# Two chained two-layer models on one core: the modulation products keep to other stages, and the value products of the neighbourhood attention take their PSUM tiles from the projections' pool

## The chip, the cores and the metric

The kernel runs on one core of one Trainium2 chip. The metric is the device time of one execution in microseconds (us). The core has TensorE (PE, with its weight load PEld), VectorE (DVE), ScalarE (ACT), GpSimd (POOL), and SyncE (SP), whose queue issues most DMAs.

## The reference

`x` is 512 tokens by 1024 features. The first model has two layers, each of them a mixer, a cross-attention to 256 memory tokens and a feed-forward stage with a causal convolution of width 3. The second model has two layers too, with a context of 256 tokens beside `x`; its norms are modulated by vectors that are computed from `c` and `c_ctx`:

```python
for l in range(2):                                     # first model
    x = x + (even_mixer, odd_mixer)[l](rms(x, mix_g[l]))   # retention + HGRN2; dilated attention
    x = x + cross_attention(rms(x, xa_g[l]), rms(mem, xm_g[l]))
    gate, up = split(rms(x, ffn_g[l]) @ w_in[l])
    x = x + (gelu(causal_conv(gate)) * up) @ w_out[l]
for i in range(2):                                     # second model
    mod   = split6(silu(c)     @ ada_w[i] + ada_b[i])  # shift, scale, gate, twice: j = 0..5
    mod_c = split6(silu(c_ctx) @ ada_w[i] + ada_b[i])
    h, hc = modulate(rms(x), mod), modulate(rms(ctx), mod_c)
    y, yc = (ab_mixer, cd_mixer)[i](h, hc)             # token MLP + neighbourhood attention;
    x   = x + g_m * y                                  #   Fourier mix + gated linear attention
    x   = x + g_f * swiglu(modulate(rms(x), mod))
    if i == 0:                                         # the context runs to the end of layer 0
        ctx = ctx + gc_m * yc; ctx = ctx + gc_f * swiglu(modulate(rms(ctx), mod_c))
return rms(x)
```

In the neighbourhood attention every query attends to 8 rows of a grid 64 wide (16 columns of each) and to the 256 context tokens, with one softmax over both.

## The kernel before

**Layout and stages.** Activations lie feature-major, as 8 tiles of 128 features by 512 tokens in fp32. The stages follow each other as mix0, xa0, ffn0, mix1, xa1, ffn1 (first model), bm0, bf0, bm1, bf1, out (second model): mixers are mix0, mix1, bm0 and bm1, feed-forward stages ffn0, ffn1, bf0 and bf1. Every fp32 product is three matmuls in fp32r: high part by high part, high by low, low by high.

**Weight units.** A unit is 512 KB of weights: one DMA on SP's queue (4 buffers `wr`), a cast on ScalarE to the high part `wh` (L303, 3 buffers), a subtraction on VectorE for the low part `wl` (L304, 3 buffers), and then 24 matmuls of 128x512 into a PSUM tile. The matmuls' lines are L322, L352, L949, L1183, L1194 and L1208, one for each kind of projection.

**PSUM.** There are two pools of four banks. `PM()` gives the tiles `m` of projections, `PA()` the tiles `a` of everything else (attention logits, transposes, sums over features, broadcasts).

**The modulation products.** The vectors `mod` and `mod_c` of both layers are 12 products (l = 0, 1; j = 0 to 5). Each reads 16 tiles of 256 KB from `w_ada` through SP's queue and accumulates on VectorE: L1070 for the first tile of a half, L1072 for the seven others, once per stream (both streams for l = 0 and for j below 2). Then VectorE transposes and sums (L1076, L1078), one small matmul folds the parts (L452), and VectorE adds the bias (L1082). The generator `side()` runs this a step at a time: each weight unit calls `tick()`, and `tick()` takes one step. `finish_side(l)` takes all steps that are left of layer l.

**Order.** The program emits its instructions in the order of the Python code; `weave()` interleaves attention units with background jobs; a scheduler then fixes the order on each engine when the program is built. On the chip every engine takes its instructions in that order.

**The places that the change touches.** In mix0 the first eight input tiles are squared and summed on GpSimd (L523, L525), and the sum is folded over features by TensorE (L427), which the norm needs. Later in mix0 the gates of the HGRN2 heads (L578 to L588) feed prefix products over time, called trees here: TensorE's L601 starts each of them, VectorE's L611 and L612 carry them. At the end of ffn1 VectorE adds the result to x (L931) and, in the norm's sum (L438), the squares of eight tiles; TensorE's L427 folds that sum, while L1208 (the context's value projection of bm0) lies between. In bm0 a unit of neighbourhood attention (`attend`, from L1340 on) makes logits (L1351), a softmax on ACT and DVE (L1253 to L1261, L1355, L1359), transposes (L1365) with their copies to SBUF (L1367), and value products `po` (L1373); projections (L1183) are the background jobs. At the border from bf0 to bm1 the last matmuls of bf0 are left as 12 jobs, which cd_mixer emits together with the first steps of `modulate` for x. Those steps are the fold (L427), its result to all partitions (L490, L1099) and the modulated tiles (L1112, L1113, L1120; the odd ones by L1108 to L1118).

Of the kernel before, what the change touches and what calls it, by code (L numbers as in the profile page):

```python
# [235 lines left out]
class Net:  # L236
    def __init__(self, ctx, tc, a):
        self.tc, self.nc, self.a = tc, tc.nc, a
        E = ctx.enter_context
        self.cp = E(tc.tile_pool(name="cp", bufs=1))  # L240
        self.xp = E(tc.tile_pool(name="xp", bufs=9))
        self.cx = E(tc.tile_pool(name="cx", bufs=9))
        self.A = E(tc.tile_pool(name="A", bufs=NSLOT))
        self.sp = E(tc.tile_pool(name="sp", bufs=40))
        self.wr = E(tc.tile_pool(name="wr", bufs=4))
        self.wh = E(tc.tile_pool(name="wh", bufs=3))
        self.wl = E(tc.tile_pool(name="wl", bufs=3))
        self.pm = E(tc.tile_pool(name="pm", bufs=4, space=PSUM))
        self.pa = E(tc.tile_pool(name="pa", bufs=4, space=PSUM))
        self.dp = E(tc.tile_pool(name="dp", bufs=1, space=bass.MemoryType.DRAM))  # L250
        self.n = 0
        self.side = None
        self.early = []
        self.consts()
# [117 lines left out]
    def tick(self):  # L372
        if self.side is not None and next(self.side, None) is None:
            self.side = None
# [139 lines left out]
    def even_mixer(self, x, filler):  # L514
# [4 lines left out]
        for k in range(8):  # L519
            xs.append(self.split(x[k], scale=self.V("mixg0", k)))  # L520
            self.fm2_step(first, xs, k)
            sq = acc if k == 0 else self.T()
            nc.gpsimd.tensor_tensor(sq, x[k], x[k], ALU.mult)  # L523
            if k:
                nc.gpsimd.tensor_tensor(acc, acc, sq, ALU.add)  # L525
# [193 lines left out]

        hv, rv, sc, ri, gates = [], [], {}, {}, {}  # L720
        inp = {0: hg_inputs(0)}
        self.mem_prep()
# [21 lines left out]
        for h in range(4):  # L744
            jobs.append(lambda h=h: retention(h, *ri[h]))
            if h < 2:
                jobs.append(lambda h=h: ret_in(h + 2))
        self.weave(trees(), jobs, depth=4, rate=0.75)
        extra = []
        jobs = iter(filler(extra))  # L750
# [149 lines left out]
    def conv_ffn(self, l, x, st, xs, gain=None, mid=None):  # L900
# [21 lines left out]
        for p, (lo, hi) in enumerate(PARTS):  # L922
# [3 lines left out]
            for m in range(8):  # L926
                if mid is not None and p > 0:
                    next(mid, None)
                ps = self.fm1(f"w_fo{l}", m * 3 + p, hid[lo:hi])
                t = self.xp.tile([128, 512], F32, tag="x", name=f"x{self.n}")  # L930
                nc.vector.tensor_add(t, ps, x[m])  # L931
                out.append(t)
                if p == 2:
                    if gain is not None:
                        nxt.append(self.split(t, scale=self.V(gain, m)))
                    self.stat_add(st, m, t)
            x = out
        return x, st, nxt

# [13 lines left out]
    def odd_mixer(self, x, st, xs, filler):  # L953
# [17 lines left out]
        p = {}  # L971
# [63 lines left out]
        ff = filler(extra)  # L1035
        jobs = jobs[:12] + ff[:1] + jobs[12:17] + ff[1:3] + jobs[17:] + ff[3:]
        self.weave(units(), jobs, depth=3, rate=0.85)
        return self.residual("w_odo", ys, x, "xag1"), extra

# [11 lines left out]
    def ada(self, l, j):  # L1051
# [5 lines left out]
        for half in range(2):  # L1057
# [16 lines left out]
            for i in ids:  # L1074
                tr = self.T()
                nc.vector.transpose(tr, acc[i])  # L1076
                o = (i * 2 + half) * 16
                nc.vector.tensor_reduce(part[:, o:o + 16], tr.rearrange("p (b t) -> p b t", t=32), AX.X, ALU.add)  # L1078
        ps = self.PA()
        self.fold(ps, part, w, 1)  # L1080
# [105 lines left out]
    def dxs(self, wts, xs, n=512, pss=None, s=None):  # L1186

        pss = pss or [self.PM() for _ in wts]
        s = s or slice(0, n)
        for j, (xh, xl) in enumerate(xs):  # L1190
            ws = slice(j * 128, j * 128 + 128)
            for ps, wt in zip(pss, wts):
                for i, (A, B) in enumerate(((wt[0], xh), (wt[0], xl), (wt[1], xh))):
                    self.nc.tensor.matmul(ps[:, s], A[:, ws], B[:, s], start=j == 0 and i == 0, stop=j == len(xs) - 1 and i == 2)  # L1194
        return pss

    def tm_c(self, w, g, cs, evac):
# [74 lines left out]
    def ab_mixer(self, x, st, c, cs):  # L1272
# [73 lines left out]
        def attend(hp, i, logits, nbias, vals, yh, yl, n, order):  # L1346
# [22 lines left out]
            yield  # L1369
            po = self.PA()  # L1370
            for s, vv in enumerate(vals):
# [190 lines left out]
    def cd_mixer(self, r):  # L1562
# [3 lines left out]
        mx = self.modulate(x, r["sx"], 1, 0, 0, xs)  # L1566
        for i, job in enumerate(r["jobs"]):
            job()
            if i in (2, 5):
                next(mx, None)  # L1570
        self.run(mx)
        SCf, SCb = self.T(), self.T()
# [32 lines left out]
        qs, ks, kcs = [], [], []  # L1605
        pq = self.dxs([self.wt("w_cd", m) for m in range(2)], xs)
        self.run(mc)
        for m in range(2):
# [310 lines left out]
def body(ctx, tc, a, stop=None, start=None):  # L1919
# [32 lines left out]
    def side(ls):  # L1952
# [4 lines left out]
        for l in ls:  # L1957
            for j in range(6):
                for _ in k.ada(l, j):
                    for _ in range(2 - l):  # L1960
                        yield True

    def finish_side(l):
        while (l, 5) not in k.done:
            k.tick()
# [3 lines left out]
    def context():  # L1969
        load("c")  # L1970
        yield
        finish_side(0)
        yield from k.ctx_in(c, cs)
# [24 lines left out]
    for step in STEPS[STEPS.index(start or "mix0"):]:  # L1998
# [6 lines left out]
        elif step == "mix1":  # L2005
            (x, st, xs), kv = k.odd_mixer(x, st, xs, lambda out: k.mem_kv(1, out))
        elif step == "bm0":
            r = k.ab_mixer(x, st, c, cs)
        elif step in ("bf0", "bf1"):
            r = k.swiglu(int(step[-1]), r)  # L2010
        elif step == "bm1":
            finish_side(1)
            r = k.cd_mixer(r)
# [27 lines left out]
```

## Time and profile before

| | |
|---|---|
| Median of 3 runs (lowest, highest) | 3136.11 us (3135.73, 3138.0) |
| The profiled execution, its span | 3135.71 us, 3133.4 us |
| TensorE busy, share of the span | 3082.6 us, 98% |
| VectorE, ScalarE, GpSimd busy | 1781.0, 1115.8, 424.6 us |
| DMA, mean over the span | 100 GB/s |

The span runs from the first to the last profiled event; the time of the execution is 2.3 us longer. All positions are microseconds from the span's start. A busy TensorE can still run at its lower clock, so busy time and granted clock are read together. `[1.00 <-POOL t L525]` behind an instruction says that its engine sat idle for 1.00 us before it, and that GpSimd's L525, which writes a tile t, ended that.

### The profile page before, as it was taken

The page shows a single profiled execution, that of the slowest core. Times are in us where ns is not written, and L with a number is a line of the kernel's source. Part 1 is how long each engine was busy: PE and PEld are TensorE (multiplying, and loading weights), DVE is VectorE, ACT ScalarE, POOL GpSimd, SP SyncE. Part 2 cuts the span into 40 slices and gives each one's busy share as a digit, 9 for nine tenths or more (in the row PEclk, how much of TensorE's full clock was granted, in tenths as well). Part 3 has the DMA queues.
Part 4 walks back from the last instruction along what each step waited for, and adds up shares of the span by engine and source line. Part 5 has one row for each costly group of instructions (what it writes and reads, how often), then busy time and mean ns, then how long its engine had stood idle before and what let it go on. Part 6 is the DMA issues. An engine that isn't in the chain of part 4 may idle for free. (4 is left out here: it accounts for less than half of the span.)

```text
span 3133.4 us, 41147 instructions
## 1 busy us (share of the span) xinstructions
PE 3082.6 (98%) x16364; PEld 2584.5 (82%) x16364; DVE 1781.0 (57%) x2916; ACT 1115.8 (36%) x1868; POOL 424.6 (14%) x369
## 2 busy tenths in 40 slices
PE   8999999999999999999999999999999999999998
PEld 6878888888877888888878777888888878888887
DVE  7767676565648767668663557443332463643333
ACT  2234353232445534423243544221212352442223
POOL 5023111010111121101021112000000310110001
PEclk9999999999999999999999999999999999999999
DMA  5224323333333422334443013232211131222232
GB/s 171 79 77 155 118 78 117 119 123 123 118 105 100 148 94 95 125 129 144 139 150 106 26 38 105 98 118 71 90 66 54 68 113 31 64 77 100 94 101 68
DMA packets 110354, 312.80 MB, mean 100 GB/s; under 512 B 12177, under 2 KB 17682, under 8 KB 110162
## 3 DMA queue, kind: packets, MB, share of 16 engines
q1 hardware_dynamic: 101968, 297.32, 28.2%
q10 hardware_dynamic: 8194, 12.86, 1.3%
q8 instruction: 129, 2.11, 0.3%
q14 instruction: 63, 0.52, 0.0%
HBM read 306.98 MB, written 3.15 MB: 99 GB/s over the span
## 5 line engine op out<-in xcount | busy, mean ns | idle before, releaser
L1183 PE MATMUL m<-t,wh 128*128 128x512 f32 (+1 forms) x3716 | 993.3, 354 | 1.1 <-DVE t L1120 0.4
L303 ACT CAST wh<-wr 128x1024 fp32r<-128x1024 f32 (+2 forms) x462 | 471.1, 1022 | 1203.5 <-PE m L1183 395.1
L304 DVE TENSOR_TENSOR wl<-wr,wh 128x1024 fp32r<-128x1024 f32 (+2 forms) x462 | 558.8, 1210 | 447.4 <-ACT wh L303 428.8
L322 PE MATMUL m<-t,wh 128*128 128x512 f32 (+1 forms) x2576 | 772.2, 382 | 0.0
L1183 PEld LDWEIGHTS m<-t,wh 128*128 128x128 f32 x3716 | 655.3, 189 | 105.6 <-issue 8.8
L1183 PE MATMUL m<-t,wl 128*128 128x512 f32 (+1 forms) x1858 | 656.0, 353 | 0.5 <-DVE wl L304 0.5
L322 PEld LDWEIGHTS m<-t,wh 128*128 128x128 f32 x2576 | 474.0, 188 | 89.9 <-issue 1.0
L322 PE MATMUL m<-t,wl 128*128 128x512 f32 (+1 forms) x1288 | 490.9, 381 | 0.0
L1183 PEld LDWEIGHTS m<-t,wl 128*128 128x128 f32 x1858 | 351.1, 189 | 49.6 <-issue 1.9
L322 PEld LDWEIGHTS m<-t,wl 128*128 128x128 f32 x1288 | 242.5, 188 | 45.9 <-issue 0.7
L438 POOL TENSOR_TENSOR t<-t,t 128x512 f32<-128x512 f32 (+1 forms) x90 | 112.2, 1250 | 1163.1 <-ACT t L433 1141.4
L1072 DVE SCALAR_TENSOR_TENSOR t<-t,silc,t 128x512 f32<-128x512 f32 x280 | 219.1, 811 | 14.7 <-DMA t<-w_ada 13.9
L949 PE MATMUL m<-t,wh 128*128 128x512 f32 x704 | 217.2, 390 | 0.0
L352 PE MATMUL m<-t,wh 128*128 128x512 f32 x496 | 158.9, 400 | 7.4 <-ACT wh L303 7.4
L949 PEld LDWEIGHTS m<-t,wh 128*128 128x128 f32 x704 | 131.8, 188 | 27.4
L411 ACT CAST t<-t 128x512 fp32r<-128x512 f32 x116 | 72.0, 621 | 189.7 <-DVE t L1547 104.4
L916 POOL TENSOR_TENSOR t<-t,t 128x512 f32<-128x512 f32 x44 | 64.5, 1467 | 549.7 <-ACT t L915 532.3
L949 PE MATMUL m<-t,wl 128*128 128x512 f32 x352 | 136.9, 389 | 0.0
L1453 DVE SCALAR_TENSOR_TENSOR x<-m,modt,x 128x512 f32<-128x512 f32 (+1 forms) x75 | 50.1, 671 | 142.4 <-PE m L1183 142.2
L421 POOL TENSOR_TENSOR s<-s,nh 128x4 f32<-128x4 f32 (+2 forms) x67 | 71.2, 1064 | 406.2 <-DVE s L483 154.5
L367 PE MATMUL m<-wh,t 128*128 128x512 f32 x384 | 123.1, 396 | 0.0
L352 PEld LDWEIGHTS m<-t,wh 128*128 128x128 f32 x496 | 93.3, 191 | 26.5 <-ACT wh L303 7.4
(391 smaller groups left out, 3602.5 us busy)
## 6 DMA issues: line engine op xcount, KB each, us to landing
t<-w_ada SPq DMA_DIRECT2D x192, 256.0 KB, 3.9
wr<-w_fi SPq DMA_DIRECT2D x88, 512.0 KB, 3.3
wr<-w_gu SPq DMA_DIRECT2D x88, 512.0 KB, 3.3
wr<-w_fo SPq DMA_DIRECT2D x32, 512.0 KB, 3.3
wr<-w_dn SPq DMA_DIRECT2D x32, 512.0 KB, 3.1
wr<-w_ev SPq DMA_DIRECT2D x24, 512.0 KB, 3.3
wr<-w_xk SPq DMA_DIRECT2D x16, 512.0 KB, 3.3
wr<-w_xv SPq DMA_DIRECT2D x16, 512.0 KB, 3.2
```

What stands on the lines that cost most here:

```text
L303: nc.scalar.copy(h[:, 0:e], r[:, 0:e])
L304: nc.vector.tensor_sub(lo[:, 0:e], r[:, 0:e], h[:, 0:e])
L322: nc.tensor.matmul(ps[:, 0:n], A[:, s], B[:, 0:n], start=c == 0, stop=c == tot - 1)
L352: self.nc.tensor.matmul(ps, A[:, s], B, start=k == 0 and i == 0, stop=k == K - 1 and i == 2)
L367: nc.tensor.matmul(pss[tb], A[:, ts], B[:, s], start=(u == 0 and j == 0 and i == 0), stop=(u == nu - 1 and j == kper - 1 and i == 2))
L411: nc.scalar.copy(h[:, 0:n], src[:, 0:n])
L421: self.nc.gpsimd.tensor_tensor(r, v, self.nh[:, 0:w], ALU.pow)
L438: e.tensor_tensor(st[0][:, 0:n], st[0][:, 0:n], sq[:, 0:n], ALU.add)
L916: nc.gpsimd.tensor_tensor(y, y, rb, ALU.mult)
L949: nc.tensor.matmul(ps[:, 0:n], A[:, s], B[:, 0:n], start=c == 0, stop=c == tot - 1)
L1072: nc.vector.scalar_tensor_tensor(acc[i], r, s, acc[i], ALU.mult, ALU.add)
L1183: nc.tensor.matmul(ps[:, s], A[:, ws], B[:, s], start=j == 0 and i == 0, stop=j == last and i == 2)
```

## The change

There are six parts.

1. A flag `quiet` makes `tick()` do nothing: in mix0 from before the memory's preparation to the end of the trees, in the weave of mix1, for the second half of the last pass of ffn0 and ffn1 (m above 3 of 8), and throughout bm0.
2. In mix0, the squares of the odd tiles are computed on ScalarE; the sums stay on GpSimd.
3. The modulation products get three empty steps ahead of the fold. `side()` spaces layer 0's steps by 2 and 1 ticks in turn (before: 2), and layer 1's by 0 and 1 (before: 1), so two steps may fall on one tick.
4. The context of bm0 waits for the first three products of layer 0 only, and bm1 for the first three of layer 1; bf0 and bf1 ask for the rest of theirs. In the built order none of these calls leaves a run of products at a border.
5. At the border to bm1, x's modulation is emitted in full after job 7 of the 12 jobs (before: its steps after the folds came behind all jobs). The context's modulation is emitted inside the first two projections of bm1, behind their input tiles 2 and 5.
6. In `attend`, the value products take their PSUM tile from `PM()` instead of `PA()`.

```diff
@@ tick @@
-        if self.side is not None and next(self.side, None) is None:
+        if self.side is not None and not self.quiet and next(self.side, None) is None:
@@ even_mixer @@
             sq = acc if k == 0 else self.T()
-            nc.gpsimd.tensor_tensor(sq, x[k], x[k], ALU.mult)
+            if k % 2:
+                nc.scalar.activation(sq, x[k], AF.Square)
+            else:
+                nc.gpsimd.tensor_tensor(sq, x[k], x[k], ALU.mult)
...
+        self.quiet = True
         inp = {0: hg_inputs(0)}
         self.mem_prep()
...
         self.weave(trees(), jobs, depth=4, rate=0.75)
+        self.quiet = False
@@ conv_ffn @@
                 if mid is not None and p > 0:
                     next(mid, None)
+                self.quiet = p == 2 and m > 3
...
+        self.quiet = False
@@ odd_mixer @@
+        self.quiet = True
         self.weave(units(), jobs, depth=3, rate=0.85)
+        self.quiet = False
@@ ada @@
+        for _ in range(3):
+            yield True
         ps = self.PA()
         self.fold(ps, part, w, 1)
@@ new @@
+    def between(self, steps, js):
+        for j in js:
+            with self.tc.issue_after(self.marks[j]):
+                next(steps, None)
+    def border(self, jobs, steps, at):
+        for i, job in enumerate(jobs):
+            job()
+            if i in at:
+                next(steps, None)
+            if i == at[-1]:
+                self.run(steps)
+        self.run(steps)
@@ attend @@
-            po = self.PA()
+            po = self.PM()
@@ cd_mixer @@
-        for i, job in enumerate(r["jobs"]):
-            job()
-            if i in (2, 5):
-                next(mx, None)
-        self.run(mx)
+        self.border(r["jobs"], mx, (2, 5, 7))
...
         pq = self.dxs([self.wt("w_cd", m) for m in range(2)], xs)
+        self.between(mc, (2, 5))
         self.run(mc)
@@ side, finish_side, context, the steps @@
-                for _ in k.ada(l, j):
-                    for _ in range(2 - l):
+                for i, _ in enumerate(k.ada(l, j)):
+                    for _ in range(i % 2 if l else 2 - i % 2):
                         yield True
-    def finish_side(l):
-        while (l, 5) not in k.done:
+    def finish_side(l, j=5):
+        while (l, j) not in k.done:
...
-        finish_side(0)
+        finish_side(0, 2)
...
         elif step == "bm0":
+            k.quiet = True
             r = k.ab_mixer(x, st, c, cs)
         elif step in ("bf0", "bf1"):
+            k.quiet = False
+            finish_side(int(step[-1]))
             r = k.swiglu(int(step[-1]), r)
         elif step == "bm1":
-            finish_side(1)
+            finish_side(1, 2)
```

No engine's count of these instructions changes but for the four squares; the 192 loads of `w_ada` are spread otherwise over the stages. In SP's order, ffn0 holds 36 of them before and 39 after, ffn1 52 and 64, bm0 16 and none, bf0 40 and 56.

VectorE at the end of ffn1, before; L1070 and L1072 are modulation products, L931 adds to x, L304 makes a unit's low part, and L438 is the last addition of the norm's sum:

```order
L1070 TENSOR_SCALAR t_13458<-t_13459,silc 128x512
L1072 SCALAR_TENSOR_TENSOR t_13458<-t_13461,silc,t_13458 128x512
L1072 SCALAR_TENSOR_TENSOR t_13458<-t_13463,silc,t_13458 128x512
L931 TENSOR_TENSOR x_13557<-m_13532,x_12802 128x512
L304 TENSOR_TENSOR wl_13650<-wr_13647,wh_13649 128x1024
L1072 SCALAR_TENSOR_TENSOR t_13458<-t_13496,silc,t_13458 128x512
L1072 SCALAR_TENSOR_TENSOR t_13458<-t_13529,silc,t_13458 128x512
L931 TENSOR_TENSOR x_13590<-m_13565,x_12842 128x512
L1072 SCALAR_TENSOR_TENSOR t_13458<-t_13562,silc,t_13458 128x512
L438 TENSOR_TENSOR t_13303<-t_13303,t_13592 128x512
```

The same place after, where L938 is the addition to x, L305 the low part and L439 the norm's addition:

```order
L938 TENSOR_TENSOR x_13510<-m_13485,x_12691 128x512
L305 TENSOR_TENSOR wl_13603<-wr_13600,wh_13602 128x1024
L938 TENSOR_TENSOR x_13540<-m_13515,x_12735 128x512
L305 TENSOR_TENSOR wl_13630<-wr_13627,wh_13629 128x1024
L938 TENSOR_TENSOR x_13570<-m_13545,x_12775 128x512
L305 TENSOR_TENSOR wl_13655<-wr_13652,wh_13654 128x1024
L439 TENSOR_TENSOR t_13294<-t_13294,t_13572 128x512
```

The modulation products have left the end of ffn1, and one low part more stands ahead of the norm's addition.

Earlier in ffn1, after, VectorE between two low parts (the first two rows of this stretch are L305's and an L413, then two L1080, and six more L1082 stand ahead of these; L1080 and L1082 are the products that were L1070 and L1072):

```order
L1082 SCALAR_TENSOR_TENSOR t_12419<-t_12468,silc,t_12419 128x512
L1082 SCALAR_TENSOR_TENSOR t_12420<-t_12468,silc,t_12420 128x512
L938 TENSOR_TENSOR x_12507<-m_12476,x_11542 128x512
L1082 SCALAR_TENSOR_TENSOR t_12419<-t_12472,silc,t_12419 128x512
L1082 SCALAR_TENSOR_TENSOR t_12420<-t_12472,silc,t_12420 128x512
L1082 SCALAR_TENSOR_TENSOR t_12419<-t_12512,silc,t_12419 128x512
L1082 SCALAR_TENSOR_TENSOR t_12420<-t_12512,silc,t_12420 128x512
L1082 SCALAR_TENSOR_TENSOR t_12419<-t_12516,silc,t_12419 128x512
L1082 SCALAR_TENSOR_TENSOR t_12420<-t_12516,silc,t_12420 128x512
L305 TENSOR_TENSOR wl_12564<-wr_12561,wh_12563 128x1024
```

Fourteen L1082 and two L1080 stand between these two low parts, with three other instructions. After, ffn1 has three places with 16 products between two low parts (the others there number 3, 2 and 6) and two with 8; before, 8 was the most.

TensorE at the end of the first units of the neighbourhood attention, after; L1195 is a projection, L1381 the logits, L1395 the transposes and L1403 the value products:

```order
L1195 MATMUL m_14619<-t_13303,wl_14591 128x256
L1381 MATMUL a_14501<-t_14326,t_14325 128x256
L1381 MATMUL a_14501<-t_14327,t_14325 128x256
L1395 MATMUL a_14532<-ident,t_14406 128x128 x4
L1395 MATMUL a_14539<-ident,t_14407 128x128 x4
L1403 MATMUL m_14649<-t_14537,t_13863 64x128
L1395 MATMUL a_14546<-ident,t_14438 128x128 x4
L1395 MATMUL a_14553<-ident,t_14439 128x128 x4
L1403 MATMUL m_14649<-t_14544,t_13863 64x128
L1403 MATMUL m_14649<-t_14537,t_13865 64x128
```

And before, where L1183 is the projection, L1351 the logits and L1365 the transposes:

```order
L1351 MATMUL a_14529<-t_14354,t_14352 128x256
L1183 MATMUL m_14727<-t_13597,wh_14723 128x512
L1183 MATMUL m_14727<-t_13598,wh_14723 128x512
L1183 MATMUL m_14727<-t_13597,wl_14724 128x512
L1183 MATMUL m_14727<-t_13599,wh_14723 128x512
L1183 MATMUL m_14727<-t_13600,wh_14723 128x512
L1183 MATMUL m_14727<-t_13599,wl_14724 128x512
L1183 MATMUL m_14727<-t_13601,wh_14723 128x512
L1183 MATMUL m_14727<-t_13602,wh_14723 128x512
L1183 MATMUL m_14727<-t_13601,wl_14724 128x512
L1365 MATMUL a_14560<-ident,t_14434 128x128 x4
```

Before, a projection lies between the logits and the transposes; after, transposes follow the logits at once and value products lie among them.

## Rows read from the trace of the kernel before

**Rows 1.** The page: busy time of TensorE, share, instructions.

```profile
PE 3082.6 (98%) x16364; PEld 2584.5 (82%) x16364; DVE 1781.0 (57%) x2916; ACT 1115.8 (36%) x1868; POOL 424.6 (14%) x369
```

**Rows 2.** TensorE's waits: waiting line, releaser; us in total, times, longest.

```profile
PE a L427 <- DVE t L438: 10.1, 7, 2.5
...
PE a L1351 <- ACT t L1258: 4.4, 5, 1.3
PE a L601 <- DVE t L588: 3.3, 1, 3.3
PE a L452 <- DVE s L470: 2.6, 3, 1.8
```

**Rows 3.** Five windows: us, TensorE busy, granted clock, DMA share, GB/s.

```profile
65.90:72.50 6.60, 5.80 (x25) 0.50 0.26 82
720.00:800.00 80.00, 80.00 (x355) 1.00 0.29 97
960.20:963.40 3.20, 3.20 (x10) 0.50 0.00 0
1608.70:1615.30 6.60, 6.60 (x20) 0.50 0.61 203
1720.00:1930.00 210.00, 204.64 (x1369) 1.00 0.20 63
```

**Rows 4.** Timeline of the start: start us, us, instruction, idle before and releaser.

```profile
7.72 2.06 DVE L304 TENSOR_TENSOR wl<-wr,wh 128x1024 fp32r<-128x1024 f32 x1
...
8.78 2.15 POOL L525 TENSOR_TENSOR t<-t,t 128x512 f32<-128x512 f32 x1
...
31.61 1.05 PE L427 MATMUL a<-c,t 128*128 128x1 f32 x8 [1.00 <-POOL t L525]
...
33.27 1.22 DVE L304 TENSOR_TENSOR wl<-wr,wh 128x1024 fp32r<-128x1024 f32 x1
```

**Rows 5.** Timeline of VectorE and TensorE where the trees of mix0 start.

```profile
64.92 0.75 DVE L1072 SCALAR_TENSOR_TENSOR t<-t,silc,t 128x512 f32<-128x512 f32 x1
...
66.41 0.98 PE L601 MATMUL a<-t,t 128*128 128x128 f32 x3 [3.25 <-DVE t L588]
```

**Rows 6.** Timeline of VectorE and TensorE in mix1.

```profile
954.79 2.45 DVE L1072 SCALAR_TENSOR_TENSOR t<-t,silc,t 128x512 f32<-128x512 f32 x2 [1.28 <-DMA t<-w_ada]
...
958.96 0.25 PE L452 MATMUL a<-s,fold 128*32 128x4 f32 x8 [1.81 <-DVE s L470]
```

**Rows 7.** Timeline of VectorE and TensorE at the end of ffn1.

```profile
1603.47 2.57 DVE L1072 SCALAR_TENSOR_TENSOR t<-t,silc,t 128x512 f32<-128x512 f32 x2
...
1605.38 0.39 PE L1208 MATMUL m<-wl,t 128*128 128x512 f32 x1
1608.25 1.09 PE L427 MATMUL a<-c,t 128*128 128x1 f32 x6 [2.48 <-DVE t L438]
```

**Rows 8.** Timeline of VectorE and TensorE at the border from bf0 to bm1.

```profile
2494.94 0.74 DVE L1112 SCALAR_TENSOR_TENSOR t<-x,modt,a 128x512 f32<-128x512 f32 x1
...
2496.16 0.58 PE L427 MATMUL a<-c,t 128*128 128x1 f32 x4 [1.66 <-DVE t L438]
...
2497.77 0.43 PE L490 MATMUL a<-ident,s 128*128 128x128 f32 x2 [0.46 <-POOL s L421]
```

**Rows 9.** Timeline of ScalarE and VectorE in ffn1, two successive weight units.

```profile
1519.99 1.05 ACT L303 CAST wh<-wr 128x1024 fp32r<-128x1024 f32 x1 [4.39 <-PE m L322]
...
1523.67 1.41 DVE L1072 SCALAR_TENSOR_TENSOR t<-t,silc,t 128x512 f32<-128x512 f32 x2
1525.43 1.05 ACT L303 CAST wh<-wr 128x1024 fp32r<-128x1024 f32 x1 [0.95 <-PE m L322]
```

**Rows 10.** Groups of the attention of bm0, 1715 to 1905: busy us, mean ns, idle before.

```profile
L1367 ACT COPY t<-a 128x512 f32<-128x512 f32 x32 | 17.6, 590 | 10.9 <-PE a L1365 9.6 <-issue 1.1
...
L1258 ACT ACTIVATE t<-t,s 128x256 f32<-128x256 f32 x32 | 16.3, 510 | 34.1 <-DVE s L1255 30.1 <-issue 3.9
...
L1359 DVE TENSOR_SCALAR t<-t,s 128x512 f32<-128x512 f32 x32 | 15.3, 479 | 0.1
```

More of the change, by code (lines that the diff above doesn't have):

```diff
@@ L1036, in odd_mixer @@
         jobs = jobs[:12] + ff[:1] + jobs[12:17] + ff[1:3] + jobs[17:] + ff[3:]
+        self.quiet = True
         self.weave(units(), jobs, depth=3, rate=0.85)
+        self.quiet = False
         return self.residual("w_odo", ys, x, "xag1"), extra
@@ L1189, in dxs @@
         s = s or slice(0, n)
+        self.marks = []
         for j, (xh, xl) in enumerate(xs):
@@ L1193, in dxs @@
                 for i, (A, B) in enumerate(((wt[0], xh), (wt[0], xl), (wt[1], xh))):
-                    self.nc.tensor.matmul(ps[:, s], A[:, ws], B[:, s], start=j == 0 and i == 0, stop=j == len(xs) - 1 and i == 2)
-        return pss
+                    m = self.nc.tensor.matmul(ps[:, s], A[:, ws], B[:, s], start=j == 0 and i == 0, stop=j == len(xs) - 1 and i == 2)
+            self.marks.append(m.ins)
+        return pss
+    def between(self, steps, js):
[10 more added lines that the diff above has]
+        self.run(steps)
     def tm_c(self, w, g, cs, evac):
```

## The prediction

> **What bounds the kernel now.** The page's busy times come first: TensorE works for 3082.6 us of a span of 3133.4 us [rows 1], so 50.8 us, 1.6%, is all the idle time there is, and the other engines matter only where TensorE waits for them. No matmul is added or removed, so the change can win only from that idle time and from one thing that busy time hides, the clock. The windows show it: in a quiet stretch of ffn0 the granted clock is 1.00 (2.4 GHz), and behind three waits it is 0.50 (1.2 GHz) for 6.6, 3.2 and 6.6 us [rows 3]. TensorE then takes twice as long for its work, so such a stretch costs half its length: 3.3, 1.6 and 3.3 us. Each wait has therefore two prices, itself and the slow stretch after it.
>
> The list of waits then says for whom TensorE waited: VectorE's L438 (10.1 us in 7), the attention's exponentials L1258 (4.4 us in 5), L588 (3.3 us) and L470 (2.6 us in 3) [rows 2]. The timelines around the longest of each kind show what VectorE did instead, and at three of them it was modulation products, 0.7 us each. These products have nothing to do with the stage in which they run; any stage with a free VectorE could take them.
>
> The sum is made against the profiled execution, 3135.71 us, which is 0.4 us under the median of the three runs, 3136.11; its span is 3133.4 us and 2.3 us lie outside.
>
> **The change, part by part.**
>
> *Start of mix0.* The sum of squares ends late and L427 waits 1.00 us for GpSimd's L525 [rows 4]. With four of eight squares on ScalarE, GpSimd has four instructions less in front of that addition, and such an instruction takes 1 to 2 us there (L525: 2.15 [rows 4]): the wait goes. The first low part L304 takes 2.06 us while GpSimd's L525 runs and 1.22 us at 33.27, when no large GpSimd instruction runs [rows 4], and TensorE waits at that moment; if GpSimd is idle there, up to 0.8 us goes as well. I take −1.5, with bounds 0 (ScalarE's squares delay its casts as much) and −2.2.
>
> The Trainium skill, page "SBUF — State Buffer", section "Who interferes with whom", says that a VectorE instruction with two SBUF inputs contends with a GpSimd instruction that reads SBUF, the loser being blocked whole. The trace agrees as far as 2.06 against 1.22 us goes; by the blocking rule the 0.8 us would go in full or not at all, so the part would be −1.8 or −1.0.
>
> *Trees of mix0.* TensorE reaches the first tree and waits 3.25 us for L588, in front of which VectorE has two L1072 [rows 5] and, just ahead of these, two more. After, no product stands there: VectorE's queue holds only the gates and low parts. Four L1072 at 0.71 to 0.75 are 2.9 us, so nearly the whole wait goes, and with it the slow stretch of 6.6 us, worth 3.3. What is late next is the pair L611 and L612 of each head, with some 1.2 us of small waits of the size that stands there already. 3.3 + 3.3 − 1.6 for what is left = 5: I take −5, bounds −6.5 and 0 (another gate late by as much).
>
> *Memory and mix1.* In mix1 L452, the fold of a product, waits 1.81 us, for a chain that begins with a wait of VectorE for `w_ada` (1.28 us) [rows 6]; the slow stretch behind it costs 1.6. After, three empty steps stand between the products and the fold, and twice as many matmuls of L322 ahead of it in the order, 23 instead of 11. That is 3.4 us; the other projections are drawn from the same fillers, so I give back 0.4: −3, bounds −5.5 (small waits around the attention units go too) and +1. In the memory's projections of mix0 more products run than before (10 loads instead of 8, and none in the trees), but the folds come later: −1, bounds −2 and +1.
>
> *End of ffn1.* TensorE's last L1208 is done at 1605.8 and L427 starts at 1608.25 after 2.48 us of waiting; meanwhile VectorE has three L1072, 3.3 us, ahead of the addition [rows 7]. After, none of the products stands behind m = 3. What stands in front of L438 instead is one low part, 1.22 us. So the chain after the last matmul of w_fo is that low part, the addition to x and L438 (0.7 each, as the products of the same shape) and between them ScalarE's square (0.6, as the copy of that shape in rows 10): 3.2 us. TensorE's cover is 13 L1208 matmuls of 0.227 us (a unit's 5.44 us [rows 9] by its 24 matmuls): 2.95 us. A wait of 0.25 is left. The wait of 2.5 and the slow stretch, 3.3, go: −5.5, bounds −6 and −3 (the low part falls at the worst place and the clock drops all the same for half the time).
>
> *Border from bf0 to bm1.* The wait of 1.66 us at L427 and of 0.46 at L490 are the context's statistics [rows 8]; after, 48 matmuls of bm1's projections of x lie ahead of that fold, since x's modulation starts earlier: the first L1112 stands at 2494.94 [rows 8], behind all the jobs, and would move ahead of the last four. The 2.1 us go, and one more that the modulation itself costs: −3, bounds −4 and −1. The context's own modulated tiles stay late.
>
> *The products' new places in ffn1.* Here the change adds. Their total is the same 192 loads, but in ffn1 up to 16 products stand between two low parts. Casts in ffn1 follow each other by 5.44 us (1519.99 and 1525.43) [rows 9], which is the time of a unit. With three buffers a low part may be made from when TensorE leaves the unit three before; so a cluster that follows low part u has until three units later, 16.3 us, when u+1 is used. VectorE then needs the cast 1.05, low part u 1.22, 16 × 0.71 = 11.3, three other instructions of 0.7 = 2.1, and low part u+1, 1.22: 16.9 us. That is 0.6 us late at a place with three others and 2.7 at the one with six. Three such places give 0.6 + 0 + 2.7 = 3.3; as VectorE had been ahead at the start of some, I take +2, bounds 0 and +9 (each wait also followed by a slow stretch).
>
> *Attention of bm0.* Before: waits for L1258 of 4.4 us in five [rows 2], at a clock of 1.00 over the stretch with 5.4 us idle [rows 3]. After, no unit waits for a PSUM slot that its own value products hold, so some of it goes; but less projection work stands between a unit's logits and its transposes. A unit's chain is the reduction, addition, exponential, scaling and the hand-overs, and of these alone the exponentials take 2 × 0.51, the scaling 0.48 and the copy 0.59 [rows 10]; all together about 4 us, while the order leaves 2.7 to 6 us of TensorE's work at the ends of groups. I take +0.5, bounds −4 (all of it gone) and +6.
>
> The Trainium skill, page "TensorE: Matmul & The Clock Gate", section "A second HAM failure mode: psum-queue depth-cycling", tells of a kernel in which short idle times between groups of matmuls, as PSUM buffers are cycled, made the clock swing and cost throughput. In this trace the five waits of bm0 left the clock at 1.00 [rows 3], so the sum takes nothing for it; by that rule a finer alternation would lower the clock here, which is the first rival.
>
> The sum: −1.5 − 5 − 3 − 1 − 5.5 − 3 + 2 + 0.5 = −16.5. Some gains may overlap with a wait that was hidden, so I round to −16: 3119.7 against the profiled execution, 3120 against the median.
>
> **The rivals.**
>
> *A new wait in bm0, slower.* Place: the six groups of attention units. Transposes now stand right behind logits. If the softmax of the last unit and the copies of 0.59 us [rows 10] are not done, TensorE has nothing else in its order; a wait as in rows 6 and 7 (1.8 to 2.5) becomes 4 us and is followed by a slow stretch as at 960.2, 1.6 [rows 3]. Six times 5.6 = 34, less the 6 that are lost there now: +28; with the other gains (−17) that is +11 or 3147. It decides from waits of about 3 us per group on. Against it: most transposes belong to units whose logits are far back. Chance 0.07.
>
> *Clusters make low parts late in ffn1.* If VectorE has no lead at the five places with 8 to 16 products, each costs 1.5 to 3 and a slow stretch of 1.6: some 16 us, all of the gain: 3135. For it: 16.9 against 16.3. Against it: between two clusters VectorE has nearly nothing else to do in 5.44 us per unit, and catches up. Chance 0.14.
>
> *The next wait takes the place.* At the trees, in mix1 and at the end of ffn1 the wait removed is followed by the next thing that VectorE has queued, half of each wait stays, and the clock still falls: 3 + 1.5 + 3 us of gain, less 2 for the clusters: −5.5, 3130. For it: VectorE has low parts and additions of its own at each. Chance 0.19.
>
> *The products do not leave.* Then nothing changes but the start and the border: 3132; the built order speaks against it, as no product stands in the three places. Chance 0.02.
>
> **How the numbers follow.** The forecast, 3120, has 0.58; its own range is 3111 to 3128, from adding about half of the parts' bounds. The range that is to hold 8 times in 10 is 3110 to 3134: it takes in the third rival and all but the slow end of the second. Faster by over 0.2%, which is 6.3 us and about what a measurement of this kernel can tell from no change, is below 3129.8; slower is above 3142.4. The forecast gives 0.56 faster and 0.02 within; the next wait in place of the old one 0.12 and 0.07; the clusters 0.05, 0.06 and 0.03 slower; the new wait in bm0 0.02, 0 and 0.05; products that stay 0, 0.01 and 0.01. Together 0.75, 0.16 and 0.09.
>
> **What would show it.** Right: no wait of L601 for L588 above 1.5 us and a clock of 1.00 around 66; no wait at L427 at the end of ffn1 above 0.5; the list of waits without L452 for L470; TensorE's idle time near 38 us; the first matmul's wait unchanged. Wrong: waits of the projections' matmuls for low parts in ffn1 (the clusters), new waits of transposes L1365 for ScalarE or VectorE in bm0 above 10 us in all, or a clock below 0.95 in that stretch.

## The result and the profile after

The kernel after takes 3157.2 us (median of 4 runs, 3156.62 to 3157.73), before 3135.9 us: 1.0069 times as long, 95% interval 1.0054 to 1.0084. The forecast was 3120, faster. The change makes the kernel 21 us slower. Stages and waits below are read from the one profiled execution of each kernel.

The page's busy times (the row that answers to [rows 1]):

```profile
PE 3094.1 (98%) x16364; PEld 2587.9 (82%) x16364; DVE 1769.7 (56%) x2916; ACT 1117.2 (35%) x1872; POOL 418.0 (13%) x365
```

TensorE has the same 16364 matmuls and is busy 11.5 us longer; the span has grown from 3133.4 to 3154.7 us. So half of the loss is idle time and half is time in which the same matmuls ran slower. To find the stages, take the same instruction of TensorE in both traces (a fold over features stands at nearly every border) and subtract its positions. The difference, after minus before, goes like this:

| Up to | Difference, us | Change in this stretch | Forecast |
|---|---|---|---|
| first fold of mix0 | −3.5 | −3.5 | −1.5 |
| end of the trees of mix0 | −9.8 | −6.3 | −5 |
| ffn0 starts | −8.3 | +1.4 | −1 |
| mix1 starts | −7.8 | +0.6 | 0 |
| mix1 ends, ffn1 starts | −10.7 | −3.0 | −3 |
| late in ffn1 (context's fold) | −3.6 | +7.1 | +2 |
| bm0 starts | −9.6 | −6.0 | −5.5 |
| bm0 ends | +22.5 | +32.1 | +0.5 |
| bf0 ends | +25.1 | +2.6 | 0 |
| border to bm1 passed | +21.8 | −3.3 | −3 |
| end | +21.0 | −0.8 | 0 |

Six of the forecast's eight terms are right within 3 us. ffn1 is off by 5, and bm0 by 32. Without bm0 the change would have gained 11.

TensorE's waits after, the answer to [rows 2] (lines shift: L427 is L428, L438 is L439, L1258 is L1288, L1351 is L1381, L1365 is L1395, L1367 is L1397, L1373 is L1403):

```profile
PE a L1381 <- ACT t L1288: 7.3, 8, 2.1
...
PE a L428 <- DVE t L439: 5.9, 4, 2.0
PE a L1395 <- ACT t L1288: 4.5, 6, 1.8
PE a L1395 <- ACT t L1397: 2.7, 2, 2.0
PE m L323 <- DVE wl L305: 2.2, 2, 1.8
PE m L1403 <- ACT t L1397: 1.5, 3, 0.9
PE a L1395 <- DVE t L1389: 1.4, 1, 1.4
...
PE m L1195 <- DVE t L1406: 0.7, 1, 0.7
```

The waits that were to go are gone or halved: L601 for L588 has no successor here, and the folds wait 5.9 us in place of 10.1. In their place stand the attention's lines: logits L1381 and transposes L1395 wait for the exponentials L1288 and the copies L1397. The last row is the only wait of a projection for a bank that a value product held (L1406 reads it): 0.7 us.

The clock, in windows as in [rows 3] (us, TensorE busy, granted clock, DMA share, GB/s): the first is in ffn1, the others in bm0.

```profile
1557.30:1564.00 6.70, 6.00 (x14) 0.50 0.41 119
1721.10:1727.70 6.60, 5.36 (x23) 0.50 0.24 79
1772.30:1778.90 6.60, 5.67 (x27) 0.50 0.15 40
1806.50:1813.10 6.60, 4.95 (x16) 0.50 0.07 26
1905.40:1915.40 10.00, 9.55 (x62) 0.50 0.00 0
```

Before, bm0 ran at 1.00 (its attention in [rows 3], the whole stage in the third window of the first experiment). Now the clock falls to 0.50 (1.2 GHz) four times there, for some 30.7 us together, which costs half, 15.4. The trace behind the first of these falls, TensorE:

```profile
1718.69 1.13 PE L1381 MATMUL a<-t,t 64*128 64x256 f32 x4 [0.16 <-ACT t L1288]
1721.61 1.11 PE L1395 MATMUL a<-ident,t 128*128 128x128 f32 x4 [1.79 <-ACT t L1288]
1723.46 1.12 PE L1395 MATMUL a<-ident,t 128*128 128x128 f32 x4 [0.73 <-ACT t L1397]
```

This is the order piece of the change section, seen on the chip: logits, and at once transposes, with no projection between. The transposes are not those of these logits: they read tiles of an earlier unit. Their own input comes from L1389; what ends their wait is an exponential, which reads a bank of logits, so they wait for a bank of `PA()`.

Ahead of the third fall the trace shows why the exponentials were late. Their input is complete with L1285; next in ScalarE's order stands the cast of a weight unit, which waits for a projection of TensorE:

```profile
1801.49 0.16 DVE L1285 TENSOR_TENSOR s<-s 128x1 f32<-128x1 f32 x1
...
1803.59 0.62 ACT L304 CAST wh<-wr 128x512 fp32r<-128x512 f32 x1 [3.57 <-PE m L1195]
1804.11 0.50 ACT L1288 ACTIVATE t<-t,s 128x256 f32<-128x256 f32 x1
...
1805.21 0.70 PE L1381 MATMUL a<-t 64*128 64x256 f32 x2 [1.55 <-ACT t L1288]
```

### The profile page after: what moved, and what is told of

It reads as the page before. It is cut to its first block, busy times and chain, and to the rows that moved or that the text cites. A ratio compares the mean times of both kernels' runs of the same rounds, so it can differ in the third digit from the quotient of the medians.

```text
span 3154.7 us, 41150 instructions
## 1 busy us (share of the span) xinstructions
PE 3094.1 (98%) x16364; PEld 2587.9 (82%) x16364; DVE 1769.7 (56%) x2916; ACT 1117.2 (35%) x1872; POOL 418.0 (13%) x365
## 5 line engine op out<-in xcount | busy, mean ns | idle before, releaser
L1195 PE MATMUL m<-t,wh 128*128 128x512 f32 (+1 forms) x3716 | 988.7, 354 | 2.4 <-ACT t L1572 0.9
L304 ACT CAST wh<-wr 128x1024 fp32r<-128x1024 f32 (+2 forms) x462 | 471.2, 1022 | 1214.4 <-PE m L1195 407.8
L305 DVE TENSOR_TENSOR wl<-wr,wh 128x1024 fp32r<-128x1024 f32 (+2 forms) x462 | 553.2, 1199 | 443.8 <-ACT wh L304 425.7
L1195 PEld LDWEIGHTS m<-t,wh 128*128 128x128 f32 x3716 | 655.9, 189 | 107.0 <-issue 5.0
L1195 PE MATMUL m<-t,wl 128*128 128x512 f32 (+1 forms) x1858 | 654.7, 352 | 0.5 <-DVE wl L305 0.5
L1195 PEld LDWEIGHTS m<-t,wl 128*128 128x128 f32 x1858 | 351.2, 189 | 49.7 <-issue 1.2
L439 POOL TENSOR_TENSOR t<-t,t 128x512 f32<-128x512 f32 (+1 forms) x90 | 110.0, 1224 | 1203.0 <-ACT t L434 1180.9
L1082 DVE SCALAR_TENSOR_TENSOR t<-t,silc,t 128x512 f32<-128x512 f32 x280 | 214.8, 802 | 15.9 <-DMA t<-w_ada 14.8
```

Source lines behind the costliest of these rows:

```text
L304: nc.scalar.copy(h[:, 0:e], r[:, 0:e])
L305: nc.vector.tensor_sub(lo[:, 0:e], r[:, 0:e], h[:, 0:e])
L439: e.tensor_tensor(st[0][:, 0:n], st[0][:, 0:n], sq[:, 0:n], ALU.add)
L1082: nc.vector.scalar_tensor_tensor(acc[i], r, s, acc[i], ALU.mult, ALU.add)
```

## Experiments

Theories at the start. **A**: bm0 is longer because the value products take their tiles from `PM()`. **B**: bm0 is longer because it has lost its modulation products and its queues start otherwise. After the first four runs A was split. **C**: the pool acts through the order alone, which leaves too little work of TensorE between a tile's logits and its own transposes. **D**: the pool's banks cost by themselves on the chip. For C the built order can be counted: the sum of TensorE's issue intervals between a tile's logits and its transposes, 48 tiles in all. Before, no tile has under 6.0 us; after, eight have (2.7 to 5.8). That count is of the order and is not a measured time.

**Undo the sixth part.**

```diff
-            po = self.PM()
+            po = self.PA()
```

> The change without its sixth part: the value products take their PSUM tile from PA() again, all else as after. Theory A (the pool is what makes bm0 32 us longer): bm0 goes back to about the length it had before, so the time is that of after less 30 to 34, about 3125 us, 0.4% under before; no wait of the transposes for the softmax above 1 us. Theory B (bm0 is longer because it has no modulation products and starts at another phase of the queues): the time stays near 3155.

Measured: 3122.05 us, 0.9955 (0.9942 to 0.9969) of before. bm0 takes 310.7 us in place of 346.9, and the rest is as after within 3 us. That is 35.2 under after, just beyond the 30 to 34 that A expected. Three windows of bm0 give the account; first after:

```profile
1605.60:1952.50 346.90, 325.71 (x1877) 0.96 0.22 69
```

then this run:

```profile
1604.00:1914.70 310.70, 306.69 (x1875) 1.00 0.24 77
```

then before:

```profile
1614.90:1930.00 315.10, 308.04 (x1885) 1.00 0.25 80
```

Idle time is 21.2 us after and 4.0 here: 17.2 us of the 36.2. Busy time is 19.0 us longer after, of which 15.4 is the clock and 3.6 stays unexplained. The waits of this run in bm0:

```profile
PE a L1381 <- ACT t L1288: 2.5, 3, 1.2
PE m L1257 <- DVE t L1132: 1.3, 1, 1.3
```

No transposes wait. Theory A holds. In the built order no tile has under 6 us between its logits and its transposes, as before the change.

**The sixth part alone**, in the kernel before.

```diff
-            po = self.PA()
+            po = self.PM()
```

> The kernel before with the sixth part alone: value products in tiles of PM(). Theory A: bm0 gets 28 to 34 us longer, 3136 + 31 = 3167 us, with waits of the transposes and logits for the softmax of 15 us more than before and a clock at its lower level in bm0 in at least three stretches. Theory B: 3136, no change in bm0.

Measured: 3171.62 us, 1.0111 (1.0097 to 1.0124). bm0 goes from 315.1 to 352.2 us, 3 us more than A's range, and no other stage moves by more than 1.5 us. The window of bm0, this run:

```profile
1615.40:1967.60 352.20, 328.24 (x1884) 0.96 0.22 72
```

Its waits are 23.5 us in place of 6.8, and the clock falls six times in it, for 30.6 us. Theory A again. In the built order the same eight tiles as in after have under 6 us, though modulation products run here.

**Modulation products in bm0 again.**

```diff
-            k.quiet = True
             r = k.ab_mixer(x, st, c, cs)
```

> After, without the flag in bm0: modulation products may run ahead of the attention of bm0 again, value products still in PM(). Theory A: within 3 us of after, 3157. Theory B: about 3125, the loss in bm0 goes.

Measured: 3168.76 us, 1.0107 (1.0093 to 1.0121). B falls. A's number is missed too: bm0 is 6.2 us longer than after, the border to bf0 17.9 us longer (26.4 in place of 8.5) and bf0 12.4 shorter. With the value products in `PM()`, the flag in bm0 is worth 11.6 us.

**Layer 1's products spaced by one tick.**

```diff
-                    for _ in range(i % 2 if l else 2 - i % 2):
+                    for _ in range(1 if l else 2 - i % 2):
```

(with the value products in `PA()`)

> The change without its sixth part, and with layer 1's products spaced by one tick as before (no two steps on one tick). In the built order no more than 8 products stand between two low parts of ffn1, instead of 16. If the 7 us lost in ffn1 come from the place with 16 products and six other instructions, this is 6 to 7 us under the run with the value products in PA() alone: about 3118. If they come from the larger number of products in ffn1 as such, there is no difference beyond 2 us: about 3125.

Measured: 3124.29 us, 0.9960 (0.9948 to 0.9973), the same as the first experiment or a little more. ffn1 is 5.2 us shorter, 321.8 in place of 327.0 (before: 322.5); its windows, first those of the first experiment, then of this run:

```profile
1241.29:1568.30 327.01, 324.30 (x1457) 1.00 0.39 134
...
1240.33:1562.17 321.84, 321.84 (x1439) 1.00 0.35 122
```

The idle time of 2.7 us, for late weight parts at a cluster, is gone. That the clusters are all that ffn1 lost is not shown: the spacing also leaves only 44 of the 64 loads of `w_ada` in ffn1 (before: 52), so clusters and number changed together, and some fold matmuls moved with them. bm0 is 7.8 us longer, though TensorE's order in its attention differs only at one place, near 1750; 5 of it is one stretch at the lower clock later on, of this run:

```profile
1840.40:1850.40 10.00, 10.00 (x28) 0.50 0.00 0
```

Around this stretch the order is the same in both runs. Why the clock falls here and not in the first experiment is open; waits in bm0 are 6.4 us here and 3.8 there.

**Value products in `PM()`, rate 1.0.** `weave()` keeps `depth` attention units in work, gives each a step per round, and then emits `rate` background jobs.

```diff
-        self.weave(units(), jobs, depth=4, rate=0.85)
+        self.weave(units(), jobs, depth=4, rate=1.0)
```

> After, value products still in PM(), but the background jobs of the attention weave at a rate of 1.0 instead of 0.85. In the built order 4 of the 48 tiles then have under 6 us of TensorE work between logits and transposes, where after has 8 and before none. Theory C (the pool only acts through the order: too little work between logits and transposes): bm0 loses 10 to 22 us against the run with PA(), so the time is 3132 to 3144, and the waits stand at the tiles with the short distance. Theory D (tiles in the projections' pool cost by themselves, by banks that come free late on the chip): 3153 to 3160 as after.

Measured: 3143.06 us (9 runs, 3139.36 to 3147.83), 1.0023 (1.0013 to 1.0033). bm0 is 334.3 us: 23.6 over the first experiment where after is 36.2 over it. The time is in C's range, bm0 1.6 over it. All value products are in `PM()` as after, and no projection waits for a bank that one of them held (0.7 us in after), so D has nothing on its side. But C's other half is missed: the waits do not stand at the four short tiles. In this run's bm0 they are for banks again:

```profile
PE a L1381 <- ACT t L1288: 7.5, 7, 2.0
PE a L1395 <- ACT t L1288: 4.7, 3, 2.7
```

None is of a transpose for its own input (L1389). In after it is one, of 1.37 us; the other seven short tiles pass without a wait.

**Value products in `PA()`, but an order with little between.**

```diff
-        self.weave(units(), jobs, depth=4, rate=0.85)
+        self.weave(units(), jobs, depth=3, rate=1.0)
```

> Value products in PA(), but three units at a time and a rate of 1.0: the background jobs are used up early, and 14 of 48 tiles have under 6 us between logits and transposes, at the end of the attention. Theory C: waits of the transposes for the softmax and of the logits for the exponentials as in after, with a lower clock in bm0; 25 to 45 us over the run with PA(), 3147 to 3167. Theory D: no loss, 3119 to 3126.

Measured: 3148.39 us, 1.0036 (1.0023 to 1.0050). bm0 takes 338.6 us without a single tile in `PM()`. Its waits (of bm0, this run) are of the kinds of after:

```profile
PE a L1381 <- ACT t L1288: 10.3, 7, 2.9
PE a L1395 <- DVE t L1389: 3.1, 2, 1.7
PE a L1395 <- ACT t L1288: 2.7, 4, 1.7
PE a L1381 <- DVE t L1348: 2.1, 1, 2.1
```

So an order can lose nearly as much without the pool. Of C the first half stands, as far as these runs go: the one line acts through the order. The second half, the distance from a tile's logits to its own transposes, does not carry the loss in after: it does not grow with the count of short tiles (4, 8 and 14 tiles: 23.6, 36.2 and 27.9 us over the first experiment), and only here do transposes wait for their own input in more than one place (3.1 us). Which property of an order decides, these runs leave open.

**Five units at a time**, with `PA()`; and the same with the spacing of the fourth experiment.

```diff
-        self.weave(units(), jobs, depth=4, rate=0.85)
+        self.weave(units(), jobs, depth=5, rate=0.85)
```

> Value products in PA(), five units at a time: no tile under 6.6 us, and most over 9. Theory C: the waits in bm0 (2.5 us in the run with PA()) shrink or stay, the clock stays at 1.00 there: 3117 to 3122. Theory D: 3122.

Measured: 3126.44 us, 0.9968 (0.9956 to 0.9981): missed by 4. bm0 is 316.3 us, with a slow stretch of 3.4.

> Value products in PA(), layer 1's products spaced by one tick, and five units at a time. In the run with that spacing alone ffn1 gained 5 us and bm0 lost 8, with one slow stretch of the clock in bm0. If that slow stretch comes from waits in the attention, more work between logits and transposes removes it: 3112 to 3117. If it comes from elsewhere: 3124.

Measured: 3121.13 us, 0.9952 (0.9940 to 0.9964): between the two guesses. ffn1 keeps its 321.8, bm0 is 319.1 with a slow stretch of 3.4 us only. More distance between logits and transposes than depth 4 gives buys nothing: bm0 is 5.6 us longer than in the first experiment, and as long as in the fourth. These runs don't explain it.

**No flag in mix0's trees and the ends of ffn0 and ffn1**, with `PA()`.

```diff
-        self.quiet = True
         inp = {0: hg_inputs(0)}
...
-                self.quiet = p == 2 and m > 3
```

> Value products in PA(), without the flag in mix0 (trees) and in the last pass of ffn0 and ffn1, so that modulation products stand there again, at somewhat other places than before. If the products on VectorE were the cause of the waits there, L605 waits again for VectorE at the first tree (1 to 3 us, with a slow stretch of 3.4) and the end of ffn1 gets about 5 us longer; 8 to 12 us in all, less up to 5 for fewer products in ffn1: 3126 to 3134. If something else took those waits away: 3122.

Measured: 3160.94 us, 1.0076 (1.0062 to 1.0090): the direction is that of the products, the size three times the guess. The trees cost 5.9 us again, with this wait, close to the one in [rows 5]:

```profile
63.44 2.05 PE L605 MATMUL a<-t,t 128*128 128x128 f32 x8 [3.45 <-DVE t L592]
```

ffn1 is 14.3 us longer and its end 9.9, bm0 another 10.9. Without the flag the kernel is 39 us slower, though before had products at these places and lost only 12 there (6.3 and 6.0 in the table). The run does not put them back where they were: the ticks are used up earlier, ffn1 holds 83 loads of `w_ada` in the built order in place of 64, and two waits of 4.5 and 4.1 us for VectorE stand in the middle of it. So it shows what the flag does for the trees, and not what it is worth at each of the other places.

**Two more orders for bm0**, both with `PA()` and the spacing by one tick: depth 5 at rate 0.7, and depth 4 at rate 0.75.

> Value products in PA(), layer 1's products spaced by one tick, five units at a time, rate 0.7. No tile has under 6.6 us of work between logits and transposes. By the order theory bm0 stays within 5 us of its shortest, 311: 3114 to 3122, as the run with depth 5 and rate 0.85 or a little under it.

Measured: 3121.33 us, 0.9952 (0.9940 to 0.9965), bm0 322.3 in the profiled run with a slow stretch of 10.2 us: missed in bm0, within the range in all.

> The same with four units at a time and a rate of 0.75: one tile has 5.8 us, and the place where the clock fell in the run with the spacing alone (rate 0.85) has another distribution of background work. If the slow stretch there comes from where the background work stands, bm0 is 311 and the time 3115 to 3119; if four units always bring one such stretch, 3122 to 3125.

Measured: 3120.23 us, 0.9951 (0.9938 to 0.9965), bm0 316.3: between the two guesses. No slow stretch falls in bm0, and yet it is 5 us longer than guessed. This is the lowest median of all, but the intervals of this run, the first experiment and the two with depth 5 and spacing overlap: each is about 0.5% faster than before, and which is best is not settled.

## Why the prediction was wrong

**The step that failed** is the term for bm0, +0.5 with bounds of −4 and +6, where +32.1 was measured. Three things were wrong in it. The waits of before, L1351 for L1258, were taken as waits for a bank that the unit's own value products held, some of which would go. They are waits for a bank that logits held, since the exponentials L1258 read logits and nothing that L1351 reads, and taking the value products out of the pool did not make these banks come free sooner. Then the term set a softmax chain of about 4 us against 2.7 to 6 us of TensorE's work between a tile's logits and its own transposes. That comparison came out, with one wait of 1.4 us at the eight short distances. What it left out is the banks of `PA()` in the changed order: logits and transposes waited for the exponentials of other tiles (7.3 and 4.5 us) and for a copy (2.7), and all waits in bm0 came to 20.6 us in place of 6.8. And the price of the clock was put at nothing, because the five waits of before had left it at 1.00. It fell four times, 15.4 us.

The first rival named the place, new waits with slow stretches behind them, and 34 us at the place, against 36.2 measured with the pool undone. That its size fits is partly luck: it had 24 us of waits in six places and 10 us of clock, and there were 17 us more idle time, in 23 shorter waits, and 15 of clock. Its time, 3147, was 10 too low, 4 of it at bm0 and 6 because the other gains came to 11 and not 17. It was given 0.07, although the order showed eight tiles under 6 us where before had none; the upper end of the range, 3134, left out even this rival.

The rule on short idle times between groups of matmuls, of the Trainium skill, page "TensorE: Matmul & The Clock Gate", section "A second HAM failure mode: psum-queue depth-cycling", was set aside on the ground of the row of before. The trace after agrees with it in part: of its four windows at 0.50 three begin during waits of 1.8 to 2.1 us, and the last behind four of 0.5 to 0.7 us, but a wait of 1.37 us at 1732.44 and one of 1.26 at 1832.77 left the clock at 1.00.

**ffn1**, +2 against +7.1: the term was mis-sized. The mechanism and even the place are right. The third place with 16 products between two low parts, with six other instructions, was estimated at 2.7 us late. TensorE's two waits there, after:

```profile
1555.67 0.49 PE L957 MATMUL m<-t,wh 128*128 128x512 f32 x1 [0.73 <-ACT wh L304]
...
1558.00 0.80 PE L323 MATMUL m<-t,wl 128*128 128x512 f32 x1 [1.84 <-DVE wl L305]
```

Late by 2.6 us, and the slow stretch at 1557.3 costs another 3.4. At the other places TensorE does not wait. In the first experiment, with the same order up to here, the same two waits came without the slow stretch, and ffn1 took 327.0 us; with the spacing by one tick and fewer products it took 321.8.

**Right, and shown by undoing:** trees (−6.3; undone, +5.9). **Right, seen in the trace alone:** mix1 (−3.0), and the border to bm1 (−3.3). There the fold of the context has no wait in front of it, in place of 1.66 us [rows 8]:

```profile
2531.62 0.50 PE L428 MATMUL a<-c,t 128*128 128x1 f32 x4
```

The end of ffn1 (−6.0 forecast as −5.5) is the same: TensorE goes from the last L1238 to the fold without the wait of 2.48 us [rows 7], and the clock stays at 1.00 until 1721:

```profile
1601.76 0.39 PE L1238 MATMUL m<-wh,t 128*128 128x512 f32 x1
1602.12 1.02 PE L428 MATMUL a<-c,t 128*128 128x1 f32 x8
```

Taking the flag away brought a wait back at this fold, 2.79 us for L439; the rest of the 9.9 us there is mostly 24 matmuls of the projection that stand ahead of the fold in that run.

**The start**, −3.5 against −1.5 with a bound of −2.2. The first low part takes 1.22 us in place of 2.06 [rows 4], and the wait for GpSimd is gone:

```profile
7.63 1.22 DVE L305 TENSOR_TENSOR wl<-wr,wh 128x1024 fp32r<-128x1024 f32 x1
...
28.14 1.05 PE L428 MATMUL a<-c,t 128*128 128x1 f32 x8
```

The 0.8 us for one low part was counted once, and a later one of the start was slow before as well (2.06 at 11.40). TensorE's waits for low parts there were 2.4 us in two before and are 0.3 after; with the 1.00 us for GpSimd that is 3.1 of the 3.5. That low parts are slow beside GpSimd's work is as the Trainium skill's page "SBUF — State Buffer" has it in "Who interferes with whom", though no run here changed GpSimd's work alone.

**The memory's projections**, −1 against +1.4. Most of this is a new wait in mix0, behind the trees. Ahead of a head's norm VectorE has three products, where before it idled for 2.33 us; the norm's GpSimd step and TensorE's L491 come late:

```profile
202.91 3.11 DVE L1082 SCALAR_TENSOR_TENSOR t<-t,silc,t 128x512 f32<-128x512 f32 x3
...
210.54 0.65 PE L491 MATMUL a<-ident,s 128*128 128x128 f32 x4 [1.10 <-POOL s L422]
```

So products that leave the trees cost something at their next place, which the forecast had at nothing. **bf0**, 0 against +2.6, has 56 loads of `w_ada` in place of 40; 1.1 us of it are waits that before did not have, 0.9 of them for ScalarE's L1572. No run took this apart.

## What to carry to other kernels

When a change moves tiles between PSUM pools, compare the built order first, on all engines: what each bank waits for before it comes free, and what stands ahead of that instruction on its own engine. The shortest distances between a producer's matmuls and the matmuls that need their result showed here that the order had changed, and neither where it would wait nor how much. A wait that leaves the clock up in one order may take it down in another, so the upper end of a range needs each new wait with its slow stretch. And of a change in many parts, cost the one part that alters the tightest stage on its own: here one line lost 35 us, and the rest of the change gained 14.

## What was not expected of the hardware

The same waits in the same order can leave the clock up or take it down. Up to the end of ffn1 the first experiment and the kernel after have the same instructions in the same order on TensorE, VectorE, ScalarE and GpSimd. At the cluster in ffn1 TensorE waits 0.74 and 1.83 us in the first experiment, and 0.73 and 1.84 after. The clock falls to 0.50 after, and not in the first experiment:

```profile
1556.52 0.50 PE L957 MATMUL m<-t,wh 128*128 128x512 f32 x1 [0.74 <-ACT wh L304]
1558.86 0.50 PE L323 MATMUL m<-t,wl 128*128 128x512 f32 x1 [1.83 <-DVE wl L305]
1555.00:1562.00 7.00, 4.43 (x19) 1.00 0.23 75
```

It is the same with the fourth experiment and the last (depth 4 at rate 0.75). The order on these engines is equal up to here, and TensorE waits 1.53 and 1.54 us at L491 just before the window; the clock stays up in the fourth and falls in the last:

```profile
253.70:256.90 3.20, 3.20 (x15) 1.00 0.47 164
253.70:256.90 3.20, 3.20 (x9) 0.50 0.47 164
```

The mean granted clock of the executions of the kernel before reaches from 0.993 (3142.6 us) to 0.996 (3130.4 us). In its trace, 6.8 us of waits in bm0 left the clock at 1.00, while single waits of 1.81 to 3.25 us elsewhere were followed by a fall [rows 3, 5, 6 and 7]. What tips it stays open, and a difference of a few microseconds between two profiled executions can be one slow stretch more or less. The 36 us of bm0 are not of this kind: the line moved it by as much in two kernels, and the medians with it.
